# A running maximum over NaN-strewn rows: three buffers made into one ring

## The chip, the cores and the metric

One core of one Trainium2 chip runs the kernel. The time is device time in microseconds of one execution, smaller is better; three runs of the kernel before gave 1252.7, 1252.75 and 1253.27 us. The engines that work here are ScalarE (ACT), GpSimd (POOL) and VectorE (DVE); SyncE (SP) issues all DMAs.

## What is computed

```python
def setup_inputs():
    batch, seq, dim = 32, 2048, 2048
    x = np.random.randn(batch, seq, dim).astype(np.float32)
    mask = np.random.rand(batch, seq, dim) < 0.1
    x[mask] = np.nan
    return {"x": x, "axis": -1}

def reference(x, axis):
    return np.nanmax(x, axis=axis).astype(np.float32)
```

65,536 rows of 2048 floats (536.87 MB) are read, a tenth of the values are NaN, and of each row the largest value that is not NaN is written (0.26 MB).

## The kernel before

**Tiles.** The rows are spread over the 128 partitions, 512 rows to each. Work is counted in *quarter rows*: Q = 512 values, 2 KB in a partition, 256 KB over all. There are 2048 of them. TILES (L16) lists the work by hand, one entry a tile: the loads of the tile, the pieces it is cut into, and the reduces, all in quarter rows. Most tiles are one load of 28, pieces of 7, 9 and 12, and reduces of 16 and 12 (4 and 3 rows). Every eighth or so gives one piece of 7 to another engine, and towards the end loads and pieces become smaller, down to one quarter.

**A piece goes through four stages.**
1. *Load.* SP issues the DMA into one of three buffers of 28 quarters (`xts`, BUFS, L304). It waits until the last reduce of the tile three before is done (`free`, L433).
2. *Key.* ACT reads the upper 16 bits of each value as an integer and writes a 16-bit key, by one Prelu whose two slopes keep numbers apart from NaNs (L375). Keys lie in one of three buffers of 12 quarters (`kts`, KEYS, NKEYS). A key instruction waits for its load, and for the back passes of the keys that lay in its buffer (`kold`); the last key of a tile also waits for those of the next buffer (L372 to 374).
3. *Back.* The key is turned again (times -1, plus TOP) and written over the upper 16 bits: numbers come out as they were, NaNs as a large negative number. POOL does nearly all of this (`pool`, L396). A piece with a minus sign in TILES is done by ACT instead (`act`, in `release`, L348).
4. *Reduce.* DVE takes the maximum over whole rows of the buffer (L421) into `accs`, one value a row. It waits for the back passes of the pieces it covers.

At the end, rows that held nothing but NaN are found and given a NaN (`find`), and six stores write the result; they stand behind all loads in SP's queue.

**The order** is written out by hand: `Order.add` (L154) issues an instruction with its waits on semaphores; a wait that an earlier instruction of that engine has already implied is dropped (`needed`, `unseen`). Each engine works its queue in order, so an instruction that waits holds up all that stand behind it on its engine. Pool and DVE instructions each raise one semaphore, loads take turns among LANES = 14 of them.

In the profile the lines of the helpers stand for their callers: L226 is every ACT instruction (kt<-xt a key, xt<-kt a back pass), L236 every back pass on POOL, L243 every reduce on DVE, L307 the issue of a load.

Of the kernel before, what the change touches and what calls it, by code (L numbers as in the profile page):

```python
# [8 lines left out]
D = 2048  # L9

Q = D // 4

TILES = (  # L16
    [([4], [4], [4])]
    + [([28], [7, 9, 12], [16, 12])] * 7
    + [([28], [9, 12, -7], [8, 20])]
    + [([28], [7, 9, 12], [16, 12])] * 7  # L20
    + [([28], [9, 12, -7], [8, 20])]
    + [([28], [7, 9, 12], [16, 12])] * 7
    + [([28], [9, 12, -7], [8, 20])]
    + [([28], [7, 9, 12], [16, 12])] * 7
    + [([28], [9, 12, -7], [8, 20])]
    + [([28], [7, 9, 12], [16, 12])] * 7
    + [([28], [9, 12, -7], [8, 20])]
    + [([28], [7, 9, 12], [16, 12])] * 7
    + [([28], [6, 10, 12], [16, 12])] * 3
    + [([28], [7, 9, 12], [16, 12])]  # L30
    + [([28], [6, 10, 12], [16, 12])] * 3
    + [([28], [7, 9, 12], [12, 16])] * 2
    + [([28], [7, 10, 11], [12, 16])]
    + [([28], [6, 10, 12], [16, 12])] * 3
    + [([28], [8, 11, 9], [8, 8, 12])]
    + [([20, 8], [11, -6, 6, 5], [16, 12])]
    + [([20, 8], [12, (-4, 7), 5], [8, 8, 12])]
    + [([17, 11], [12, (-4, 6), 6], [4, 12, 12])]
    + [([16, 12], [11, -5, 5, 7], [16, 12])]
    + [([13, 15], [9, -4, 7, 8], [12, 8, 8])]  # L40
    + [([14, 14], [9, -4, 4, 4, 7], [12, 8, 8])]
    + [([11, 10, 7], [5, 6, (-3, 7), 7], [4, 4, 4, 8, 8])]
    + [([11, 9, 8], [4, 7, (-2, 7), 6, -2], [4, 4, 4, 8, 8])]
    + [([8, 7, 6, 7], [3, 5, 7, (3, -3), 3, 4], [8, 4, 8, 8])]
    + [([6, 5, 6, 5, 6], [5, (5, -1), (-1, 5), 5, 3, 3], [4, 4, 4, 4, 4, 4, 4])]
    + [([5, 6, 5, 4, 4, 3, 1], [(-2, 3), 3, 3, (4, -1), 4, 4, -2.0, 2], [4, 4, 3, 1, 4, 4, 4, 4])]
    + [([4, 4, 3, 2, 4, 2, 3, 3, 3], [2, 2, 4, (-2.0, 1), 2, 3, 3, (-1, 2), (1, -1, 1), 2, -1.0], [4, 4, 4, 4, 4, 4, 4])]
)

GROUPS = [TILES[i : i + 15] for i in range(0, 60, 15)] + [TILES[60:73], TILES[73:]]  # L50


# [3 lines left out]
APART = (70, 71, 72, 73)  # L56
WIDE = 7
BUFS = 3

KEYS = 3 * D  # L60
NKEYS = 3
# [3 lines left out]
LANES = 14  # L65


# [10 lines left out]
def total(pieces):  # L78
    return sum(sum(map(abs, p)) if isinstance(p, tuple) else abs(p) for p in pieces)


def joints(pieces, reds):

    flat = []
    at = 0  # L90
    for step, parts in enumerate(pieces):
        for c in parts if isinstance(parts, tuple) else (parts,):

            flat.append((at, at + abs(c), c < 0, step + isinstance(c, float)))
            at += abs(c)
    needs = []
    done = 0
    for n in reds:
        over = [i for i, (a, b, _, _) in enumerate(flat) if a < done + n and b > done]
        done += n  # L100
        pools = [i for i in over if not flat[i][2]]
        backs = [i for i in over if flat[i][2]]
        if pools and backs and flat[pools[-1]][3] > flat[backs[-1]][3]:
            backs = []
        needs.append(pools[-1:] + backs[-1:])
    pairs = {}
    for need in needs:
        if len(need) == 2 and all(sum(i in n for n in needs) == 1 for i in need):
            for i in need:
                pairs[i] = tuple(need)  # L110
    return pairs
# [61 lines left out]
def kernel(  # L173
# [6 lines left out]

# [14 lines left out]
    rows = [sum(sum(loads) for loads, _, _ in g) * Q // D for g in GROUPS]  # L203
    assert R == P * sum(rows)
# [8 lines left out]
    xts = [sing.tile([P, WIDE * D], i32, name=f"xt{i}") for i in range(BUFS)]  # L213
    kts = [sing.tile([P, KEYS], u16, name=f"kt{i}") for i in range(NKEYS)]
    accs = sing.tile([P, sum(rows)], f32, name="acc")
    nones = flag.tile([P, sum(rows)], i32, name="none")
    late = sing.tile([P, rows[LATE]], i32, name="late")

    with tc.tile_critical():  # L219
        order = Order(nc)  # L220

        def act(deps, pair=None, **kw):
            return order.add(
                "act",
                nc.scalar,
                lambda: nc.scalar.activation(**kw),  # L226
                deps,
                lane=pair,
                joint=pair is not None,
            )  # L230

        def pool(deps, pair=None, **kw):
            return order.add(
                "pool",
                nc.gpsimd,
                lambda: nc.gpsimd.tensor_scalar(**kw),  # L236
                deps,
                lane=pair,
                joint=pair is not None,
            )  # L240

        def dve(deps, do, **kw):
            return order.add("dve", nc.vector, lambda: do(**kw), deps)  # L243
# [26 lines left out]
        act([e_warm], out=warm, in_=warm, func=ACT.Prelu, alpha=0.5)  # L270

        free = [[] for _ in range(BUFS)]
        kfree = [[] for _ in range(NKEYS)]
        clock = 0

        def last(uses):

            return list({back: e for back, _, e in sorted(uses, key=lambda u: u[1])}.values())

        key = 0  # L280
        used = KEYS
        number = 0
        lanes = [[] for _ in range(LANES)]
        turn = 0
        stores = []
        ready = []
        flagged = 0
        r0 = 0
        for gi, (s, g) in enumerate(zip(rows, GROUPS)):
            xg = xr[r0 : r0 + P * s].rearrange("(p s) d -> p (s d)", p=P)  # L290
            og = of[r0 : r0 + P * s].rearrange("(p s) -> p s", p=P)
            r0 += P * s
            first = sum(rows[:gi])
            acc = accs[:, first : first + s]
            base = 0
            for loads, pieces, reds in g:
                assert sum(loads) == total(pieces) == sum(reds)
                xt, before = xts[number % BUFS], free[number % BUFS]
                number += 1
                landed = []  # L300
                at = 0
                for c in loads:
                    c *= Q
                    e = order.add(  # L304
                        "sp",
                        nc.sync,
                        lambda: nc.sync.dma_start(  # L307
                            out=xt[:, at : at + c], in_=xg[:, base + at : base + at + c]
                        ),
                        before + lanes[turn],  # L310
                        lane=f"load{turn}",
                        step=16,
                    )
                    lanes[turn] = [e]
                    turn = (turn + 1) % LANES
                    landed.append((at, at + c, e))
                    at += c
                clean = []
                after = []
                at = done = 0  # L320
                reds = [n * Q for n in reds]
                part = []
                held = []
                pairs = {}
                if number not in APART:
                    pairs = joints(pieces, [n // Q for n in reds])
                flat = sum((p if isinstance(p, tuple) else (p,) for p in pieces), ())
                half = {}
                piece = 0

                def cleaned(a, b, k, i, e):

                    nonlocal clock
                    clock += 1
                    both = [(a, b, k, flat[i] < 0, clock)]
                    if i in pairs:
                        if pairs[i] not in half:
                            half[pairs[i]] = both
                            return
                        both += half.pop(pairs[i])  # L340
                    for a, b, k, back, when in both:
                        kfree[k].append((back, when, e))
                        clean.append((a, b, e))

                def name(i):
                    return f"pair{number}_{pairs[i][0]}" if i in pairs else None

                def release():  # L348
                    for a, b, k, kp, e, i in held:
                        e = act(  # L350
                            [e],
                            name(i),
                            out=xt[:, a:b].bitcast(i16)[:, 1::2],
                            in_=kp,
                            func=ACT.Copy,
                            bias=float(TOP),
                            scale=-1.0,
                        )
# [139 lines left out]
```

## Time and profile before

The profiled execution took 1252.86 us, of which 1251.1 us are the span from the first to the last instruction.

| | |
|---|---|
| median of the runs | 1252.75 us |
| profiled execution; its span | 1252.86 us; 1251.1 us |
| loads | 105, of them 61 of 28 quarters (7168 KB) |
| HBM read, mean rate over the span | 536.87 MB, 429 GB/s |
| keys on ACT | x247, 913.3 us, idle before them 278.3, of which 258.3 for a DMA |
| back passes on POOL | x236, 1167.3 us, idle before them 77.9 |
| back passes on ACT | x24, 52.9 us |
| reduces on DVE | x175, 1107.6 us (and one of part of a row), idle before them 136.6 |

Busy time of the engines, DMA share and rate in some stretches (us from the start of the span):

| stretch | DVE | ACT | POOL | DMA share | GB/s |
|---|---|---|---|---|---|
| 801 to 1001 | 178.87 | 148.75 | 195.67 | 1.00 | 435 |
| 1001 to 1201 | 196.92 | 178.06 | 189.07 | 1.00 | 430 |
| 1201 to 1242 | 40.97 | 38.54 | 38.83 | 1.01 | 421 |
| 1240 to 1248 | 8.00 | 5.34 | 6.19 | 0.27 | 94 |

The "DMA share" is the mean busy share of the core's 16 DMA engines in the stretch. In the profile's groups, "idle before" is the idle time of the engine just before the instructions of the group, with what ended most of it. The chain of waits follows the work that ended last back from the end, at each step to what released it; the timeline lists the instructions of each engine in order, with the idle time before them in brackets.

### The profile page before, as it was taken

How to read it: one execution, taken by the hardware profiler on the slowest of the kernel's cores; microseconds unless marked ns; L12 is line 12 of the kernel's file. 1: busy time of each engine (PE TensorE's matmuls, PEld its weight loads, DVE VectorE, ACT ScalarE, POOL GpSimd, SP SyncE). 2: the span in 40 equal slices, each digit the busy share in tenths (PEclk: the TensorE clock that was granted, in tenths of full speed). 3: DMA queues.
4: the chain of work that ended last, by engine and by line, in shares of the span. 5: the costliest groups of instructions: out<-in, count | busy, mean ns of one | idle time of the engine just before them, and what ended most of it. 6: DMA issues, size and time to landing. Idle time of an engine off the chain costs nothing.

```text
span 1251.1 us, 893 instructions
## 1 busy us (share of the span) xinstructions
DVE 1110.8 (89%) x181; ACT 965.5 (77%) x273; POOL 1168.4 (93%) x242
## 2 busy tenths in 40 slices
DVE  0888989888889888898988888998888899999999
ACT  3777887778777877788777877777777778999997
POOL 2999989998999899998999899999999999989998
DMA  9999999999999999999999999999999999999997
GB/s 415 438 416 436 440 440 436 415 440 440 438 433 420 440 440 436 433 422 440 440 436 433 422 440 438 438 433 422 440 438 437 435 422 436 427 438 428 429 428 298
DMA packets 15992, 537.20 MB, mean 429 GB/s; under 512 B 2545, under 2 KB 2545, under 8 KB 3569
## 3 DMA queue, kind: packets, MB, share of 16 engines
q1 hardware_dynamic: 15984, 537.14, 99.4%
q14 instruction: 8, 0.06, 0.0%
HBM read 536.87 MB, written 0.26 MB: 429 GB/s over the span
## 4 chain that ended last, share of the span: by engine, by line
DMA 40%; DVE 29%; POOL 22%; ACT 9%; issue 1%; SPq 0%
DMA xt<-in_x_dram 40%; DVE acc L243 29%; POOL xt L236 22%; ACT kt L226 8%; ACT xt L226 1%; SPq L307 0%; DVE none L249 0%; DVE acc L263 0%; SPq L493 0%; SPq L219 0%
## 5 line engine op out<-in xcount | busy, mean ns | idle before, releaser
L236 POOL TENSOR_SCALAR xt<-kt 128x3584 int16<-128x3584 uint16 (+11 forms) x236 | 1167.3, 4946 | 77.9 <-ACT kt L226 64.0
L243 DVE TENSOR_REDUCE acc<-xt 128x3 f32<-128x6144 f32 (+4 forms) x175 | 1107.6, 6379 | 136.6 <-POOL xt L236 129.1
L226 ACT ACTIVATE kt<-xt 128x3584 uint16<-128x3584 int16 (+9 forms) x247 | 913.3, 3734 | 278.3 <-DMA xt<-in_x_dram 258.3
L226 ACT ACTIVATE xt<-kt 128x512 int16<-128x512 uint16 (+6 forms) x24 | 52.9, 2202 | 0.7
L226 ACT ACT_TABLE_LOAD x1 | 1.3, 1283 | 0.9 <-SPq L219 0.9
L243 DVE TENSOR_REDUCE xt<-xt 128x1 f32<-128x1536 f32 x1 | 1.7, 1739 | 0.0
L269 DVE MEMSET scalars<- 128x1 f32 x1 | 0.1, 59 | 1.0 <-SPq L219 1.0
L249 DVE TENSOR_SCALAR none<-acc 128x414 int32<-128x414 f32 (+1 forms) x2 | 0.8, 381 | 0.1
L263 DVE TENSOR_TENSOR acc<-acc,none 128x414 int32<-128x414 int32 (+1 forms) x2 | 0.7, 374 | 0.1
L249 POOL TENSOR_SCALAR late<-acc 128x91 int32<-128x91 f32 x1 | 0.5, 547 | 0.1
L263 POOL TENSOR_TENSOR acc<-acc,late 128x91 int32<-128x91 int32 x1 | 0.3, 342 | 0.1
L479 POOL MEMSET const-float32-0.0<- 128x1 f32 x1 | 0.1, 98 | 0.2 <-issue 0.2
L226 ACT ACTIVATE scalars<-scalars 128x1 f32<-128x1 f32 x1 | 0.2, 203 | 0.0
L479 POOL MEMSET const-bfloat16-1.0<- 128x1 bf16 x1 | 0.1, 101 | 0.0
L479 POOL MEMSET const-uint8-127<- 128x1 uint8 x1 | 0.1, 101 | 0.0
L479 POOL MEMSET const-float32-1.0<- 128x1 f32 x1 | 0.1, 98 | 0.0
## 6 DMA issues: line engine op xcount, KB each, us to landing
xt<-in_x_dram SPq DMA_DIRECT2D x61, 7168.0 KB, 22.6
xt<-in_x_dram SPq DMA_DIRECT2D x2, 5120.0 KB, 17.5
xt<-in_x_dram SPq DMA_DIRECT2D x3, 2816.0 KB, 22.6
xt<-in_x_dram SPq DMA_DIRECT2D x4, 2048.0 KB, 22.3
xt<-in_x_dram SPq DMA_DIRECT2D x5, 1536.0 KB, 29.1
xt<-in_x_dram SPq DMA_DIRECT2D x2, 3584.0 KB, 24.7
xt<-in_x_dram SPq DMA_DIRECT2D x6, 1024.0 KB, 26.8
xt<-in_x_dram SPq DMA_DIRECT2D x3, 1792.0 KB, 30.0
```

Of the source, the lines that this page charges most:

```text
L226: lambda: nc.scalar.activation(**kw),
L236: lambda: nc.gpsimd.tensor_scalar(**kw),
L243: return order.add("dve", nc.vector, lambda: do(**kw), deps)
L249: lambda: engine.tensor_scalar(out=none, in0=acc, scalar1=NONE, scalar2=float(0x00800000), op0=ALU.is_equal, op1=ALU.mult,),
L263: lambda: engine.tensor_tensor(out=bits, in0=bits, in1=none, op=op),
L269: e_warm = order.add("dve", nc.vector, lambda: nc.vector.memset(warm, 1.0), [])
L479: nc = _bacc.Bacc("TRN2", target_bir_lowering=False, num_devices=1)
```

## The change

- The three load buffers become one ring `xt` of RING = 84 quarters; a load waits for the reduces of the quarters that lay in its places 84 quarters before (`given`). LOADS, PARTS and REDS are now three separate lists over all 2048 quarters; up to quarter 1432 the loads are still one of 4 and 51 of 28, the last 616 are cut anew, 113 loads in all.
- The three key buffers become one ring `kt` of KEYS = 36 quarters. A step's keys are laid behind the last ones, or at 0 if they would not fit before the end (`room`). A key waits for the back passes whose keys lay there (`freed`). Where it has to wait for one anyway, or has no load to wait for, it takes on the waits of steps up to AHEAD = 12 quarters further on.
- The usual pieces are 8, 12 and 8 (44 times), reduced as 8, 12, 8; then three of 7, 9, 12, then others, from 6 to 16 at first, then falling to 1. No early piece goes to ACT any more; after quarter 1398 pieces marked A do ("A1": one step later; "+": in one step with the piece before).
- Four pieces, three of 9 and one of 7, marked V, have their back pass on DVE, in front of the reduce that needs it.
- LANES is 20; a store also waits for the last load's landing.

```diff
-    + [([28], [7, 9, 12], [16, 12])] * 7
-    + [([28], [9, 12, -7], [8, 20])]
...
+LOADS = (
+    []
+    + [4]
+    + [28] * 51
+    + [20, 23, 18, 23, 20, 15, 25, 24, 21, 22, 19, 22, 16, 16, 20, 14, 18, 15, 15, 10, 16, 13, 15, 11, 11]
+    + [10, 8, 9, 10, 10, 8, 7, 6, 6, 8, 8, 5, 7, 6, 6, 4, 4, 5, 3, 4, 4, 4, 2, 2, 3, 3, 3, 3, 3, 2, 1, 2]
+    + [2, 2, 2, 2]
 )
+PARTS = (
+    []
+    + ['4P']
+    + ['8P', '12P', '8P'] * 44
+    + ['7P', '9P', '12P'] * 3
+    + ['6P', '10P', '12P', '16P', '9V', '12P', '13P', '6A', '13P', '15P', '11P', '9V', '10P', '11P', '12P']
+    + ['8P', '14P', '9V', '14P', '10A', '10P', '10P', '15P', '10P', '15P', '14P', '7V', '13P', '6P', '15P']
+    + ['7A', '10P', '12P', '16P', '15P', '11P', '4A1', '+6P', '14P', '7P', '11P', '12P', '9P', '4A1', '8P']
...
+    + ['4P', '2A1', '2P', '3P', '1A', '+2P', '2P', '1A1', '3P', '3P', '1A1', '2P', '1A1', '+1P', '1P', '1P']
+    + ['2P', '2P', '2A1']
+)
+REDS = (
+    []
+    + [4]
+    + [8, 12, 8] * 44
+    + [16, 12] * 4
+    + [24, 12, 8, 8, 16, 16, 20, 20, 20, 24, 24, 20, 12, 12, 16, 20, 20, 20, 12, 12, 16, 12, 12, 12, 8, 12]
+    + [12]
+    + [12, 8, 8] * 3
+    + [8] * 6
+    + [4, 4, 8, 4, 8, 8, 4, 8]
+    + [4] * 23
+    + [2, 2, 4]
+)
...
-BUFS = 3
+RING = 84
+AT = 80
+KEYS = 36
-KEYS = 3 * D
-NKEYS = 3
-LANES = 14
+LANES = 20
+AHEAD = 12
...
+        def load(upto):
...
+                before = [given[q - RING] for q in range(a, b) if q >= RING]
...
+        def done(p, kp, e):
...
+                for k in range(kp, kp + p.b - p.a):
+                    kfree[k] = {p.engine: e}
+                    kbusy[k] = False
...
+        def reduce():
...
+                for o in mine:
+                    own.remove(o)
+                    back("dve", nc.vector, *o)
...
+        def room(at, c):
+            return 0 if at + c > KEYS else at
+
+        def freed(at, c):
+            want = {}
+            for k in range(at, at + c):
+                for who, (s, v) in kfree[k].items():
...
+                    want[s] = max(want.get(s, 0), v)
+            return list(want.items())
+
+        for i, ps in enumerate(steps):
+            a, b = ps[0].a, ps[-1].b
+            c = b - a
+            load(b)
+            key = room(key, c)
+            assert not any(kbusy[key : key + c])
+            deps = list(dict.fromkeys(landed[a:b])) + freed(key, c)
+            late_load = order.unseen("act", landed[a:b])
+            busy = order.unseen("act", freed(key, c))
+            if busy or not late_load:
+                nxt, j = key + c, i + 1
+                while j < len(steps) and steps[j][-1].b <= b + AHEAD:
+                    n = steps[j][-1].b - steps[j][0].a
+                    nxt = room(nxt, n)
+                    if any(kbusy[nxt : nxt + n]) or nxt < key + c and nxt + n > key:
+                        break
+                    deps += freed(nxt, n)
+                    nxt, j = nxt + n, j + 1
+                    if not busy:
+                        break
+            e_key = order.add(
+                "act",
+                nc.scalar,
+                lambda: nc.scalar.activation(
+                    out=kt[:, key * Q : (key + c) * Q],
+                    in_=ring(a, b).bitcast(i16)[:, 1::2],
...
+                deps,
+            )
+            kbusy[key : key + c] = [True] * c
...
+                if p.engine == "V":
+                    own.append((p, kp, e_key))
+                elif p.engine == "A":
+                    held.append([p, kp, e_key, p.behind])
+                    release(b == total)
+                else:
+                    back("pool", nc.gpsimd, p, kp, e_key)
+            key += c
+            reduce()
...
-                [e],
+                [ready[g], landed[-1]],
```

`steps` are the parts in order, those with "+" joined to the one before. `order.unseen` gives those of the waits that ACT has not had yet.

## The prediction

> **What bounds the kernel now.** I read the page's totals first, then the chain of waits in order of time, then the groups by form, then the timeline.
>
> ```profile
> span 1251.1 us, 893 instructions
> DVE 1110.8 (89%) x181; ACT 965.5 (77%) x273; POOL 1168.4 (93%) x242
> ...
> q1 hardware_dynamic: 15984, 537.14, 99.4%
> ```
>
> The loads' queue keeps the 16 DMA engines busy for 99.4% of the span; in the stretches the share drops only in the last one (0.27 of 1240 to 1248). So the kernel waits for its data up to 1242 us, and some 9 us at the end are the rest. Nothing can be won in the first 1242 us, and everything can be lost there: whatever leaves the queue empty adds to the time one for one. How near that is, the chain shows for one load of 28 quarter rows:
>
> ```profile
> 67.79 22.60 DMA xt<-in_x_dram
> 90.42 3.20 ACT kt L226
> 93.61 0.07 issue
> 93.69 4.20 POOL xt L236
> 97.89 0.08 issue
> 97.97 5.34 POOL xt L236
> 103.34 15.16 DVE acc L243 x2
> 118.51 22.63 DMA xt<-in_x_dram
> ```
>
> A load lands at T = 90.42 and its last reduce ends at 118.51, T + 28.1; only then can its buffer's next load be issued, which lands 22.6 us later. Three buffers turn in 50.7 us, so a load takes 16.93. The first load tells what a load needs when nothing is queued ahead of it:
>
> ```profile
> 0.94 50.21 SPq L307 DMA_DIRECT2D xt<-in_x_dram  x5
> ...
> 5.86 1.91 ACT L226 ACTIVATE kt<-xt 128x2048 uint16<-128x2048 int16 x1 [3.47 <-DMA xt<-in_x_dram]
> ```
>
> Issued at 0.94, used at 5.86: 4.92, of which 4 x 0.605 = 2.4 is transfer and 2.5 is fixed. So the queue stays full if a load is issued at least 2.5 before the previous one lands: by T + 2 x 16.93 - 2.5 = T + 31.4. Now the slack is 3.3 us.
>
> The prices (mean ns of one):
>
> ```profile
> L243 DVE TENSOR_REDUCE acc<-xt 128x3 f32<-128x6144 f32 x63 | 412.1, 6544 | 4.9 <-POOL xt L236 4.8
> L236 POOL TENSOR_SCALAR xt<-kt 128x6144 int16<-128x6144 uint16 x61 | 429.5, 7041 | 5.9 <-ACT kt L226 1.2
> L226 ACT ACTIVATE kt<-xt 128x6144 uint16<-128x6144 int16 x61 | 324.6, 5321 | 17.1 <-POOL xt L236 17.1
> ...
> L243 DVE TENSOR_REDUCE acc<-xt 128x2 f32<-128x4096 f32 x20 | 87.6, 4410 | 0.0
> ...
> L236 POOL TENSOR_SCALAR xt<-kt 128x4096 int16<-128x4096 uint16 x2 | 9.5, 4773 | 0.4 <-ACT kt L226 0.4
> L226 ACT ACTIVATE kt<-xt 128x4096 uint16<-128x4096 int16 x2 | 7.2, 3608 | 4.5 <-DMA xt<-in_x_dram 4.5
> ```
>
> A quarter row is 512 elements. Other sizes follow from these: a key costs 0.43 a quarter (16: 7.04, 9: 4.03), a back pass on POOL 0.57 (16: 9.32, 14: 8.18), a reduce 2.14 a row (6 rows: 12.95). ACT starts 0.03 after the POOL it waited for (POOL ends at 97.89, ACT starts at 97.92 here):
>
> ```profile
> 97.92 5.32 ACT L226 ACTIVATE kt<-xt 128x6144 uint16<-128x6144 int16 x1 [0.38 <-POOL xt L236]
> ```
>
> POOL starts 0.07 after ACT, and 0.08 after POOL.
>
> **The change, part by part.**
>
> *Load ring.* 84 quarters are the same three buffers, and a load of 28 still needs the whole load three before it reduced: 0. Small loads add 113 - 105 = 8 transfers. In the stretches 801-1001 and 1001-1242 the rate falls from 435 to 430 and 421 GB/s, that is 200 x 5/435 + 41 x 14/435 = 3.6 us for some 44 small loads, 0.08 each: +0.7. LANES 20 changes which semaphore a load counts on; the load 20 back has long landed: 0. The stores also wait for the last landing; they are issued on SP behind all loads already, and the last one has to wait for the last reduce anyway: 0, at worst one store's 1.5.
>
> *The end.* The last load is 2 quarters instead of 3; key 1.04, back on ACT 1.34, reduce 2.28, against two keys, back and the same reduce: -0.1.
>
> *Pieces 8, 12, 8 (a, b, c).* POOL does 4.77 + 7.04 + 4.77 + 3 x 0.08 = 16.82 a load (16.81 before), DVE 4.41 + 6.54 + 4.41 = 15.36 (15.16), both under 16.93. By busy time alone: 0.
>
> *Key ring and the early waits: here the cost is.* I followed the slots: from the fourth load on, b always gets 0-12, c 12-20, a 20-28 (12 does not fit behind 28), so each key piece goes where the same piece of the load before was, and eight slots stay empty. The key of b must wait for POOL's b of the load before; and as that makes it "busy", it collects the waits of the steps up to AHEAD = 12 quarters on, too: that is c, whose slots the last load's c holds, POOL's last piece of that load. So now key b waits until POOL has done *all* of the load before. That closes a loop in each load: 0.03 + key b 5.32 + 0.07 + POOL b 7.04 + 0.08 + POOL c 4.77 = **17.31**, against 16.93. POOL runs a meanwhile (0.08 + 4.77) and then idles 0.57 instead of 0.08. Queued behind the waiting key b on ACT is only key c; who is late is POOL, then the reduces, then the load three on. Before, key 12 waited for POOL's *first* piece of its own load (the 0.38 above), which closes no such loop.
>
> Walked from the start: c of load 4 ends at T + 21.6, its reduce 6.2 later, T + 27.8. Each load adds 0.38; 31.4 is reached after ten loads. c of load 44 ends at 95.1 + 40 x 17.31 = 787.5, the load this frees is issued at 793.7 and lands at 793.7 + 2.5 + 16.93 = 813.1; at the old rate it would be 801.3. Cost: **+11.8**. In the next seven loads (7, 9, 12 and 6, 10, 12, still reduced as 16 + 12) POOL keeps this lag; the reduce of 12 after that of 16 ends 1.9 later against POOL than 12 + 8 did: **+2**.
>
> *The re-divided end (from quarter 1320).* Load 49 is cut 16, 9 (back on VectorE, "9V"), ... and its first reduce is of 24. 16 waits for the last POOL of the load before (855.6); key 16 ends at 862.7, POOL at 872.1. Key 9V collects the wait of the following 12, whose slots 9-21 lie on those of 16: so it starts after POOL's 16, and ends at 876.2. The back pass on VectorE then takes 5.0 (estimate: its 128x414 tensor-scalar takes 0.593 and its 128x7 one 0.169, 1.04 ns an element), the reduce of 24 12.95: 894.1. The next load is issued there, where 883.2 - 2.5 = 880.7 was due: **+13.4**. Even with no lag this path is about 42 us from landing to reduce, against 31.4.
> After that ACT and POOL take turns, each with a similar wait: 13 (POOL done 907.0), key 15, POOL 15 (922.5), keys 9 and 10, POOL 10 (937.1), key 11, POOL 11 and 12 (955.6), key 14, then 9V behind the reduces (976.3), key 14, key and back of 10 on ACT (992.9), reduce of 24: 1005.9. This brings the reduced end from quarter 1372 to 1540 in 111.8, where loads take 168 x 0.605 = 101.6: **+10.2**. Up to quarter 1700 VectorE has reduces of 20, 12, 12, 16, 20 (behind 7V) and four times 20: 86.7 and 3.9 for V, and it waits 12.4 for POOL: 3.0 for the 10 of 1550; 1.1 for the 15 of 1585 (its key waited for the 15 before); 2.1 for the 6 of 1634 (key 13 waited for POOL's 14 until 1042.2); 1.0 for the 15 of 1640; 5.2 for the 12 of 1672 (queued behind 7A on ACT); no more for the 16. Together 103.0 (1108.9), loads take 96.8: **+6.2**. To quarter 1784 its reduces of 12, 12, 16, 12, 12, 12, 8 take 45.7, and it waits 3.2 and 5.8 for POOL's 15 and 14, whose keys waited in the same way: 54.7 (50.8): **+3.9**. From there pieces are mostly under 10, and 84 quarters hold the chain easily: 0.
>
> Sum: 1251.1 + 0.7 - 0.1 + 11.8 + 2 + 13.4 + 10.2 + 6.2 + 3.9 = 1299.2 of span. The profiled execution took 1252.86, 1.76 more than its span and within 0.1 of the median: **1301**.
>
> *V's price from both sides.* 5.0 is from the nearest row, short as it is; POOL's row for 9 is 5.34; below it, two elements a cycle would make 2.5, four times 2.5 less: 1291. A V that finds POOL at work might also have to wait for it: up to a POOL of 16, 9.3, each time.
>
> The Trainium skill speaks against V here. Its page SBUF — State Buffer (section Who interferes with whom) has it that a VectorE instruction in a two-port mode and a GpSimd one exclude each other for a whole instruction, and its page VectorE: DVE Perf Modes (section The perf-mode tier table) lets tensor_scalar run in such modes. The reduces of this trace run beside POOL without delay, so no row here shows it. By it V would take 2.5 and wait for some 4 of POOL: +1.5 each, 1307 instead of 1301.
>
> **The rivals.**
> 1. *Only the loop of 8, 12, 8 bites, the re-divided end hides its waits* (9V costs little, or POOL catches up): 1252.9 + 14.4 = 1267. For it: from 1320 POOL has only 626 of 728 quarters. Against: these waits are latency, not work.
> 2. *Only the end bites*: the loop is just as long as a load and the 3.3 of slack takes it. Then 1252.9 + some 33 = 1286. Against: 0.38 a load is far over what these rows vary by.
> 3. *No slower.* The early wait on ACT is always over when key b is due: without it, POOL would end c at T + 3.7 of the next load and key b is free at T + 3.64, so on paper the wait is 0.1 long. It decides at a loop of 16.93: if POOL's 8 or key 12 took 0.4 less than their rows, or if the wait I read into the step is not issued, the queue stays full, and likewise at the end. Then 1252.9 + 0.6 = 1253.5. For it: ACT has 23% idle. Against: every term has its row.
> 4. *V and POOL exclude each other* as far as one whole POOL instruction each time: 1301 - 10 + 4 x 7 = 1319 at most, about 1307.
> 5. *Faster* by over 0.2% needs 2.5 us out of the last 9, of which the edits touch 0.1.
>
> **How the numbers follow.** What this kernel's measurement can tell from no change is about 0.2%, 2.5 us. Forecast 0.57 (own range 1288 to 1312), rival 1 0.13, rival 2 0.09, rival 3 0.13, rival 4 0.06, rival 5 0.02. Range 1264 to 1312: it takes in rivals 1, 2 and most of 4 and V's bounds; rivals 3 and 5 and some of 4 stay out. Faster 0.02; same 0.12 (rival 3 but for 0.01); slower 0.86.
>
> **What would show it.** In the profile after: slices of some 424 GB/s (7.34 MB in 17.31 us) from the tenth on, when the slack is gone; the key of 12 waiting for POOL; POOL's 12 waiting some 0.5 for ACT in each load, and 8-12-8 repeating every 17.3 us; a hole in the DMA of over 10 us near 885-895, and a POOL idle for 7 us just before. If loads land every 16.93 all through, the loop is wrong; if there is no hole around quarter 1432, the end is. The DVE tensor-scalar of 4608 elements gives V's price.

## The result, and the profile after

The changed kernel takes 1310.3 us (median of five runs, 1310.19 to 1310.86) against 1252.94 before: 1.0458 times as long, 95% interval 1.0443 to 1.0473. Its profiled execution has a span of 1309.1 us, 58.0 more than before.

In the profile after, L467 is a key on ACT, L336 a back pass on POOL or VectorE, L358 one on ACT, L394 a reduce and L304 the issue of a load. The totals, with the DMA's busy share and its rate in 40 equal slices of 32.7 us:

```profile
span 1309.1 us, 937 instructions
DVE 1129.2 (86%) x226; ACT 952.0 (73%) x267; POOL 1156.8 (88%) x234
...
DMA  9999999999999999999999999997899999999994
GB/s 421 424 440 429 438 431 424 421 428 431 422 419 428 421 422 428 422 426 422 428 422 422 421 428 414 435 407 298 374 380 392 397 408 413 397 433 430 428 426 165
...
q1 hardware_dynamic: 17136, 537.14, 96.6%
```

The engines have hardly more to do (POOL and ACT less). The bytes are the same, but the queue of loads stands empty for 3.4% of the span instead of 0.6%. It shows in two places: from the eighth slice on the rate is mostly 419 to 428 where it was mostly 433 to 440, and from the 28th on there is a hole, 298, from which the rate climbs back only by the 36th. The last slice is nearly empty as well, 165 against 298 before. The same row of the profile before (slices of 31.3 us):

```profile
GB/s 415 438 416 436 440 440 436 415 440 440 438 433 420 440 440 436 433 422 440 440 436 433 422 440 438 438 433 422 440 438 437 435 422 436 427 438 428 429 428 298
```

The groups of instructions say who waits for whom (busy time, mean, then idle time before them and its releaser):

```profile
L336 POOL TENSOR_SCALAR xt<-kt 128x4096 int16<-128x4096 uint16 (+14 forms) x228 | 1155.8, 5069 | 143.0 <-ACT kt L467 130.2
...
L467 ACT ACTIVATE kt<-xt 128x4096 uint16<-128x4096 int16 (+12 forms) x243 | 910.8, 3790 | 342.0 <-POOL xt L336 221.4
```

Before, the keys on ACT waited 258.3 us for DMA and 19.1 for POOL; now 221.4 for POOL. And POOL waits 130.2 for ACT, 64.0 before. The waits before (us in total, how often, the longest):

```profile
POOL xt L236 <- ACT kt L226: 64.0, 65, 15.7
ACT kt L226 <- POOL xt L236: 19.1, 51, 0.8
```

Now there are two engines that wait for each other in turns: the chain of waits shows it for the main part.

```profile
406.90 5.33 ACT kt L467
412.23 0.07 issue
412.31 7.05 POOL xt L336
419.36 0.08 issue
419.44 4.76 POOL xt L336
424.20 0.02 issue
424.22 5.33 ACT kt L467
429.55 0.07 issue
429.62 7.05 POOL xt L336
```

Key of 12, POOL's 12, POOL's 8, and the next key of 12 begins 0.02 after it: 424.22 - 406.90 = 17.32 for a load that the DMA could bring in 16.93. No load stands in this chain between 78 and 780 us; before, one stood in every turn of the three buffers.

The timeline at load 49 has the second place (a line with x4 stands for four instructions in a row and has the shape of the first):

```profile
855.94 7.03 ACT L467 ACTIVATE kt<-xt 128x8192 uint16<-128x8192 int16 x1 [7.91 <-POOL xt L336]
863.05 9.28 POOL L336 TENSOR_SCALAR xt<-kt 128x8192 int16<-128x8192 uint16 x1 [7.14 <-ACT kt L467]
872.37 17.55 ACT L467 ACTIVATE kt<-xt 128x4608 uint16<-128x4608 int16 x4 [9.40 <-POOL xt L336]
876.44 2.76 DVE L336 TENSOR_SCALAR xt<-kt 128x4608 int16<-128x4608 uint16 x1 [12.46 <-ACT kt L467]
879.23 36.66 DVE L394 TENSOR_REDUCE acc<-xt 128x6 f32<-128x12288 f32 x5
```

Each line begins where the one above ends (the fourth where the first of the four keys above it, the 9, ends). The reduce of 24 quarters runs from 879.23 to 892.2, and only then is the next load issued. In the stretches (busy time of DVE, ACT, POOL; clock; DMA share; GB/s) this wait is a hole, a DMA share of 0.23:

```profile
879.40:892.40 13.00, 13.00 (x2) 12.97 (x4) 10.62 (x2) 1.00 0.23 97
```

The end of the kernel after, in the same columns:

```profile
1165.00:1240.00 75.00, 74.70 (x18) 74.84 (x28) 72.38 (x20) 1.00 1.00 430
1240.00:1282.00 42.00, 42.00 (x19) 41.90 (x31) 40.58 (x19) 1.00 1.01 424
1282.00:1290.00 8.00, 8.00 (x4) 8.00 (x11) 7.60 (x6) 1.00 0.85 346
1290.00:1309.00 19.00, 16.39 (x11) 5.25 (x6) 9.55 (x10) 1.00 0.06 14
```

The queue is full again from 1165 on, but VectorE is busy without a gap from 1168.7 on and still reduces for 17 us after the loads have ended. Before, the span ended 9 us after the last load's packets; now it is 20.

**Where the 58 us are.** From the DMA packet records of the trace I took when each load's packets end, and set it against a queue that is never empty (first packet at 1.95; 0.6024 us a quarter and 0.065 a load, fitted to the packets of before). The difference is what the queue has lost by then. The last load ends 46.2 late, 8 more loads cost 0.5, and the stretch after it is 10.9 longer: 57.6 of 58.0. The other 0.4 are the error of the fit: by it the kernel before itself ends 0.4 early.

### The profile page after: what moved, and what is told of

Read it like the earlier page. It is cut to its first block, busy times and chain, and to the rows that moved or that the text cites. A ratio compares the mean times of both kernels' runs of the same rounds, so it can differ in the third digit from the quotient of the medians.

```text
span 1309.1 us, 937 instructions
## 1 busy us (share of the span) xinstructions
DVE 1129.2 (86%) x226; ACT 952.0 (73%) x267; POOL 1156.8 (88%) x234
## 4 chain that ended last, share of the span: by engine, by line
POOL 56%; ACT 29%; DVE 12%; DMA 2%; issue 2%; SPq 0%
POOL xt L336 56%; ACT kt L467 28%; DVE acc L394 11%; DMA xt<-in_x_dram 2%; ACT xt L358 1%; DVE xt L336 1%; DVE xt L394 0%; SPq L304 0%; DVE none L242 0%; DVE acc L256 0%; SPq L544 0%; SPq L230 0%
## 5 line engine op out<-in xcount | busy, mean ns | idle before, releaser
L336 POOL TENSOR_SCALAR xt<-kt 128x4096 int16<-128x4096 uint16 (+14 forms) x228 | 1155.8, 5069 | 143.0 <-ACT kt L467 130.2
L394 DVE TENSOR_REDUCE acc<-xt 128x2 f32<-128x4096 f32 (+3 forms) x216 | 1110.7, 5198 | 163.7 <-POOL xt L336 160.0
L467 ACT ACTIVATE kt<-xt 128x4096 uint16<-128x4096 int16 (+12 forms) x243 | 910.8, 3790 | 342.0 <-POOL xt L336 221.4
L358 ACT ACTIVATE xt<-kt 128x1024 int16<-128x1024 uint16 (+6 forms) x22 | 43.2, 1963 | 0.4
L336 DVE TENSOR_SCALAR xt<-kt 128x4608 int16<-128x4608 uint16 (+1 forms) x4 | 16.0, 3999 | 12.5 <-ACT kt L467 12.5
L394 DVE TENSOR_REDUCE xt<-xt 128x1 f32<-128x1024 f32 x1 | 1.2, 1208 | 0.0
## 6 DMA issues: line engine op xcount, KB each, us to landing
xt<-in_x_dram SPq DMA_DIRECT2D x4, 3840.0 KB, 16.4
xt<-in_x_dram SPq DMA_DIRECT2D x3, 4096.0 KB, 16.4
xt<-in_x_dram SPq DMA_DIRECT2D x2, 5632.0 KB, 19.9
```

What stands on the lines that cost most here:

```text
L336: lambda: engine.tensor_scalar(out=upper(p), in0=keys(p, kp), scalar1=-1.0, scalar2=float(TOP), op0=ALU.mult, op1=ALU.add,),
L358: lambda: nc.scalar.activation(out=upper(p), in_=keys(p, kp), func=ACT.Copy, bias=float(TOP), scale=-1.0,),
L394: lambda: nc.vector.tensor_reduce(out=to, in_=xt[:, first:end].bitcast(f32).rearrange("p (c d) -> p c d", c=m), axis=mybir.AxisListType.X, ...
L467: lambda: nc.scalar.activation(out=kt[:, key * Q : (key + c) * Q], in_=ring(a, b).bitcast(i16)[:, 1::2], func=ACT.Prelu, bias=EDGE, scale= ...
```

## The experiments

My theory: all of it comes from the waits that a key takes on for steps up to AHEAD quarters further on. The rivals: the ring of 36 keys or the pieces are too tight by themselves; VectorE is late by its coarser work; every early wait costs something, whatever it waits for. The measured side in one table (losses of the queue as above, in us):

| kernel | time | lost by quarter 1432 | lost at the last load | from there to the end |
|---|---|---|---|---|
| before | 1252.9 | 0.6 | -0.4 | 9.0 |
| changed | 1310.3 | 17.1 | 46.2 | 19.9 |
| no_ahead | 1254.95 | 0.9 | 1.9 | 8.4 |
| ahead_in_the_end | 1294.3 | 0.9 | 29.9 | 19.7 |
| ahead_in_the_loop | 1271.5 | 16.3 | 18.9 | 8.4 |
| loop_7_9_12 | 1270.6 | 0.4 | 17.7 | 8.2 |
| loop_7_12_9 | 1313.4 | 44.1 | 61.2 | 8.2 |
| loop_7_9_12_at_12 | 1255.4 | 1.9 | 2.3 | 8.7 |
| only_when_busy | 1298.0 | 6.8 | 32.5 | 20.7 |
| only_when_idle | 1255.2 | 0.5 | 1.4 | 8.7 |
| ahead_1320_1784 | 1294.5 | 1.1 | 30.0 | 19.8 |
| no_ahead_no_v | 1259.5 | 1.2 | 6.1 | 8.7 |

### Without the early waits

```diff
-AHEAD = 12
+AHEAD = 0
```

> AHEAD = 0: a key waits only for the keys that lay in its own slots, nothing else is changed. Theory (the early waits close the loops): the loop of 17.31 us a load opens, 8-12-8 repeats at the rate of the loads, 16.93; the 46 us that the queue of loads stood empty go down to under 5, and with the lag the 11 us that the reduces run behind at the end go too: 1253 to 1262 us. Rival (a ring of 36 keys with these pieces is too small by itself, the early waits only name the wait first): some 1295 to 1310. Rival (the coarse reduces and VectorE's four back passes make VectorE late): 1285 to 1310.

1254.95 us, 1.0016 of before (1.0006 to 1.0025). The ring of 36 keys, the pieces, the reduces, VectorE's back passes and the 113 loads are all still there, and 55.3 of 57.4 us are gone. The timeline of the main part, where 8, 12, 8 again takes as long as a load:

```profile
607.22 16.72 POOL L336 TENSOR_SCALAR xt<-kt 128x6144 int16<-128x6144 uint16 x3 [0.20 <-ACT kt L467]
...
615.20 12.34 ACT L467 ACTIVATE kt<-xt 128x4096 uint16<-128x4096 int16 x3 [4.56 <-DMA xt<-in_x_dram]
624.12 16.72 POOL L336 TENSOR_SCALAR xt<-kt 128x6144 int16<-128x6144 uint16 x3 [0.18 <-ACT kt L467]
```

ACT's three keys of a load follow each other, and what they wait for is the load. POOL repeats after 624.12 - 607.22 = 16.90. And at load 49 the key of 9 follows the key of 16, without waiting for POOL between them:

```profile
835.57 10.96 ACT L467 ACTIVATE kt<-xt 128x8192 uint16<-128x8192 int16 x2 [4.55 <-DMA xt<-in_x_dram]
842.69 9.31 POOL L336 TENSOR_SCALAR xt<-kt 128x8192 int16<-128x8192 uint16 x1 [3.75 <-ACT kt L467]
846.91 7.69 DVE L336 TENSOR_SCALAR xt<-kt 128x4608 int16<-128x4608 uint16 x1
```

### On in one part, off in the other

```diff
-                while j < len(steps) and steps[j][-1].b <= b + AHEAD:
+                while j < len(steps) and steps[j][-1].b <= b + (AHEAD if a >= 1320 else 0):
```

> Early waits off for steps before quarter 1320, on behind it. Theory: loads land every 16.93 up to quarter 1320 (about 15 us back), the hole at quarter 1432 stays at 10 us or more, and the reduces are still some 10 us late at the end: 1292 to 1299. Rival (the end runs late only because it begins late): under 1275.

1294.28 us. The main part loses nothing, the hole behind load 51 is 9 us (0.9 to 10.0), and the reduces end late.

With `a < 1320` in place of `a >= 1320`:

> Early waits on for steps before quarter 1320, off behind it. Theory: the loop costs its 15 to 17 us as before, the end costs little more: 1266 to 1275. Rival (the end is late by its pieces, slots or VectorE's back passes, not by early waits): 1290 or more.

1271.46 us. The two parts add up: 16.5 and 39.3 over no_ahead make 55.8, where both together cost 55.35. So the end is not late because it begins late.

### The loop's sum against the load

The early waits stay on before quarter 1320 only, as in ahead_in_the_loop, and the main part is cut in another way.

```diff
-    + ['8P', '12P', '8P'] * 44
+    + ['7P', '9P', '12P'] * 44
...
-    + [8, 12, 8] * 44
+    + [16, 12] * 44
```

> As ahead_in_the_loop (1271.5), but the 44 loads are cut 7, 9, 12 and reduced 16, 12. The key of the second piece still waits for POOL's last piece of the load before. Theory (the loop's sum against the load decides, not the wait): 0.03 + key 9 4.03 + 0.07 + POOL 9 5.34 + 0.08 + POOL 12 7.04 = 16.59, under 16.93: no lag, 1254 to 1258. Rival (each early wait costs a fixed delay): 1270 as before.

1270.63 us, and this was not what I expected; but the two halves of it differ. By quarter 1432 the queue had lost 0.4 us: with the wait in place and a sum of 16.59 there is no lag, as the theory has it. The 17 were lost behind it, where no early wait is left.

With `['7P', '12P', '9P'] * 44`:

> As loop_7_9_12, cut 7, 12, 9. Theory: 0.03 + key 12 5.32 + 0.07 + POOL 12 7.04 + 0.08 + POOL 9 5.34 = 17.88, 0.95 over a load; 41 loads, nearly no slack because 16 + 12 is reduced later: about 38 us more than no_ahead, 1288 to 1297; POOL repeats every 17.88. Rival (a fixed delay a wait): 1270.

1313.41 us, 16 over the range, and 17 are lost behind quarter 1432 as in the last run (44.1 to 61.2), which the range left out. In the main part POOL's 12 begins every 17.89 us, against 17.88 from the rows:

```profile
210.06 16.74 POOL L336 TENSOR_SCALAR xt<-kt 128x6144 int16<-128x6144 uint16 x3 [1.15 <-ACT kt L467]
...
227.95 16.74 POOL L336 TENSOR_SCALAR xt<-kt 128x6144 int16<-128x6144 uint16 x3 [1.16 <-ACT kt L467]
...
245.84 16.71 POOL L336 TENSOR_SCALAR xt<-kt 128x6144 int16<-128x6144 uint16 x3 [1.16 <-ACT kt L467]
```

Three sums, 16.59, 17.31, 17.88, lost 0.4, 16.3 and 44.1 by quarter 1432. So in the main part an early wait costs nothing by itself; the loop that it closes costs what it is longer than a load, once the slack of the ring is used up.

The 17 behind quarter 1432 have another cause. With 7, 9, 12 or 7, 12, 9 from the start the keys of load 48 begin in slot 21 and not 12, and those of load 49 at 0. The first key there in loop_7_9_12, to be set beside the line at 835.57 above:

```profile
838.68 10.96 ACT L467 ACTIVATE kt<-xt 128x8192 uint16<-128x8192 int16 x2 [7.91 <-POOL xt L336]
```

It waits 7.91 for POOL, by its own slots: 0 to 16 still hold keys of the 10 and the 12 just before it. To see whether the place alone does this, loop_7_9_12 with one line more:

```diff
+            if a == 1320:
+                key = 12
             key = room(key, c)
```

> As loop_7_9_12 (1270.6), but the keys of load 48 (quarter 1320) begin in slot 12, as they do in the changed kernel; without that they begin in slot 21. In loop_7_9_12 the queue had lost 0.4 us by quarter 1432 and 17 behind it. Theory (the end's pieces fit 36 slots only from the place they were laid out for: from 21 on, the 16 of load 49 falls on the slots of the 12 before it): the loss behind 1432 goes to 2 as in no_ahead, 1253.5 to 1256. Rival (7, 9, 12 reduced as 16 and 12 come to the end later): 1268 to 1271.

1255.37 us (1.0022 of before, 1.0012 to 1.0032): 15.3 us of it were only where in the ring the keys stood. The end fits the place that it has in the changed kernel, slot 12, and not slot 21; other places were not tried, nor this one for 7, 12, 9.

### Which half of the rule

```diff
-            if busy or not late_load:
+            if busy:
```

> AHEAD = 12, but early waits are taken only by a key that has to wait for POOL anyway; a key with neither wait takes none. Theory: the loop is made by this half (the key of b is busy and takes c's wait), so 8-12-8 repeats every 17.3 and some 15 us are lost by quarter 1348; the 9 on VectorE no longer waits for POOL's 16, so the hole at 1432 shrinks from 9 to under 5: 1272 to 1295. Rival (the other half makes the loop): under 1265.

1298.02 us. Over the range, and half wrong: the main part lost 5.5 by quarter 1348, not 15, while the hole behind quarter 1432 shrank to 4.0, as expected. ACT's timeline says why (its keys wait for a load only every second time):

```profile
218.94 3.62 ACT L467 ACTIVATE kt<-xt 128x4096 uint16<-128x4096 int16 x1 [0.87 <-POOL xt L336]
225.69 3.62 ACT L467 ACTIVATE kt<-xt 128x4096 uint16<-128x4096 int16 x1 [3.13 <-DMA xt<-in_x_dram]
230.90 8.83 ACT L467 ACTIVATE kt<-xt 128x6144 uint16<-128x6144 int16 x2 [1.59 <-POOL xt L336]
243.37 8.83 ACT L467 ACTIVATE kt<-xt 128x4096 uint16<-128x4096 int16 x2 [3.64 <-POOL xt L336]
```

At 230.90 the key of 12 waits for POOL; at 243.37 a key of 8 has done so and the key of 12 behind it goes at once. Without the other half the first key of a load is itself busy in every second load; it then takes the second key's wait, for POOL's 12 of the load before, and the loop is closed in every second load only. From quarter 1432 on this half alone costs nearly as much as both: the queue loses 25.7 more (28.9 in ahead_in_the_end).

```diff
-            if busy or not late_load:
+            if not busy and not late_load:
```

> The other half: early waits only by a key that has no wait of its own. Theory: no loop in the main part (under 2 us lost by quarter 1348); the 9 on VectorE now is busy itself (the key of 16 no longer took its wait) and takes none, so most of the end's waits go too: 1254 to 1268. Rival: 1272 or more.

1255.18 us (1.0019, 1.0008 to 1.0029), as no_ahead. The harm is in the keys that wait anyway and take on more; the other half made it worse in the main part. By it the third key of a load, with no wait of its own, takes the wait of the next load's first key; so that key is never busy, and it is the second that closes the loop, in each load.

### Where the lateness at the end is made

```diff
-                while j < len(steps) and steps[j][-1].b <= b + AHEAD:
+                while j < len(steps) and steps[j][-1].b <= b + (AHEAD if 1320 <= a < 1784 else 0):
```

> Early waits only from quarter 1320 to 1784. The prediction put nothing on what comes after 1784; on the chip the reduces end 20 us after the last load there, 11 more than with no early waits. Theory (the lateness is made before 1784 and VectorE, busy all the time from there, carries it to the end): 1290 to 1294, as ahead_in_the_end (1294.3). Rival (early waits behind 1784 make it): 1279 to 1285.

1294.47 us, 0.5 over the range but as with early waits to the end (1294.28): nothing is made behind 1784, and nothing made up there.

### VectorE's back passes

AHEAD = 0, and:

```diff
-'9V'
+'9P'
...
-'7V'
+'7P'
```

> AHEAD = 0, and the four back passes on VectorE are given to POOL. Theory (VectorE's back pass holds POOL or is held by it, 2.8 to 8.3 us long where 2.2 to 2.4 is its work): VectorE gets 15 us back, POOL has the room; the queue loses 1 us less at quarter 1432, and the reduces end nearer the last load: 1252.5 to 1255. Rival (POOL becomes late by 21 us of work in the end): 1256 or more.

1259.46 us (1.0055 of before, 1.0038 to 1.0072): 4.5 us more than with V, and the rival was right. POOL's 9 now stands behind its 16, the reduce of 24 begins at 857.68 instead of 854.64, and the queue loses 4.8 by quarter 1452 (1.7 with V). Without early waits the four passes are worth their place; with them it was not tried.

## Why the prediction came out as it did

It said 1301, within 1264 to 1312, and slower; measured are 1310.3. The two places of the loss and their waits were right, one term was put at nothing, and two others missed in opposite ways.

- *The queue of loads is full, so nothing can be won and all can be lost*: nothing speaks against it. Not one of the variants is faster than the kernel before; the nearest, no_ahead, lies 0.2% above it.
- *The loop of 17.31*: right. 17.32 in the chain, POOL idle 0.57 to 0.60 before its 12 (0.57 was said), and the load freed by load 44 issued at 794.0 (793.7). The slack was gone after ten loads, as said: load 14 is the first to land late, at 244 us, but that is the eighth slice and not the tenth. Shown by AHEAD off for this part alone, and by three sums.
- *Load 49 and the reduce of 24*: right in kind. The key of 9 began at 872.37 (872.1), and the reduce ended at 892.2 instead of 894.1, because V took 2.76 and not 5.0. The hole cost 9.3 and not 13.4: the load before it landed later as well (885.0; 883.2 was said). Shown by ahead_in_the_end.
- *ACT and POOL in turns up to quarter 1784*: the reduces ended at 1005.7 for quarter 1540 (1005.9) and at 1105.4 for 1700 (1108.9). Altogether the queue lost 46.2, the sum had 47.5 (11.8 + 2 + 13.4 + 10.2 + 6.2 + 3.9). That the two lie so near is in part luck: by quarter 1432 the queue had lost 16.4 more than before, where the sum had 13.8, which makes up for 2.6 of the 4.1 that the hole was set too dear; from there to quarter 1784 it lost 19.4, against 20.3.
- *The end, -0.1, and "0" from quarter 1784 on*: this is the term that was mis-sized, by 11 us. It was right that the ring of 84 holds the chain and the queue loses nothing more there. But the reduces had then fallen further behind the loads, and this lag is hidden only as long as loads come. From the trace, the reduces up to quarter 1808 end at 1175.3; that is 32.8 after the packets of their load, in no_ahead 21.0: they are 11.8 us further behind the loads as they really came. VectorE takes 2.28 for a reduce of 4 quarters that load in about 2.5, so it makes up little: it is busy without a break to 1306 and ends 11 us later after the last load. ahead_1320_1784 shows that the lag was there before 1784. I walked the lag as far as it touched the queue and dropped it there.
- *V's price*: its lower bound, 2.5, was the nearest. The V took 2.73 and 2.76 for 4608 elements and 2.17 for 3584 when POOL was idle, 8.34 when it was not: 16.0 for the four, where the sum had 18.9.
- *Rivals*: "only the loop" (1267) and "only the end" (1286) are what ahead_in_the_loop (1271.5) and ahead_in_the_end (1294.3) measure, and neither was the case alone. "No slower" would have needed the wait to be over when its key was due; from the fourth load of 28 to the last of the main part ACT starts its key of 12 0.03 after POOL in each. *V and POOL exclude each other* is true (below), but that its 1307 lies nearest to 1310.3 is chance: the four V together were shorter than in the sum, and what was missing in the sum is the lag at the end.

Open: a ring of more keys with early waits. The variant keys_48 (KEYS = 48, AHEAD = 12; 1253 to 1270 us were expected) gave no time: with 84 quarters of loads it needs 218.5 KB a partition, and 207.9 are there. The span of no_ahead is 2.3 us longer than that of the kernel before: 0.5 are eight more loads and 2.3 small gaps in the queue (1.9 against -0.4), with half a microsecond back at the end; which waits make the gaps was not looked into.

## What to carry to other kernels

A wait taken early, to have one wait fewer later, is free only if it does not close a loop: add up the instructions that the wait now puts in a row round one turn (here key, back, back, with their hand-overs) and hold the sum against what one turn may take; busy shares do not show it, since each engine by itself had time left. Where a ring hides that a later stage has fallen behind, carry that lag to the end of the kernel: it comes due when the loads stop, if the stage is nearly as slow as the loads. And a hand-made order in a ring of slots need not fit every starting place: cutting the work before it in another way moved it, and cost 15 us.

## What was not expected of the hardware

VectorE's back pass on 16-bit keys runs at nearly twice the rate that its small tensor-scalar on 32-bit values showed (0.58 ns an element, from 2.17 us for 3584 and 2.76 for 4608, against 1.04), but in none of the traces does it run beside POOL. The changed kernel has a V that came second:

```profile
930.82 5.87 POOL L336 TENSOR_SCALAR xt<-kt 128x5120 int16<-128x5120 uint16 x1 [1.95 <-ACT kt L467]
930.93 8.34 DVE L336 TENSOR_SCALAR xt<-kt 128x4608 int16<-128x4608 uint16 x1
```

VectorE begins 0.11 after POOL and ends at 939.27, 2.58 after POOL's end at 936.69: by these times it stood still until POOL was done. In no_ahead, above, V of 9 lasts 7.69, to 854.60, again 2.60 after the end of POOL's 16 at 852.00. Later in no_ahead a V came first:

```profile
900.53 2.76 DVE L336 TENSOR_SCALAR xt<-kt 128x4608 int16<-128x4608 uint16 x1
901.44 14.18 POOL L336 TENSOR_SCALAR xt<-kt 128x5120 int16<-128x5120 uint16 x2 [2.98 <-ACT kt L467]
```

V ends at 903.29 in its usual time, and now POOL's 10, the first of the two, is the longer one: 7.61 instead of 5.87, to 909.04, 5.75 after V's end. So whichever begins second stands still, and the profile counts this as busy time. This is what the Trainium skill has on its page SBUF — State Buffer (section Who interferes with whom): the two exclude each other for a whole instruction. The traces agree. The reduces beside POOL kept their times (4.410 us for two rows before and after).
